# Half the tokens at a time from the first mixer to the choice of experts, and two token tiles' experts gathered

## The chip, the cores and the metric

The kernel runs on one core of one Trainium2 chip. The metric is device time in microseconds. A core has a matrix engine (TensorE, PE), a vector engine (VectorE, DVE), a scalar engine (ScalarE, ACT), a general engine (GpSimd, POOL), a queue engine (SyncE, SP) and 16 DMA engines. Every engine works through its own instructions in program order and waits for others by semaphores.

## The reference

Two transformer blocks over 512 tokens of width 1024, in fp32, cut to what matters here:

```python
# first block, modulated by mod = silu(c) @ w_mod + b_mod
h = rms_norm(x) * (1 + sc1) + sh1
x = x + 0.5 * gt1 * rms_norm(swiglu(h, w_gate1, w_up1, w_down1))      # 1024 -> 2816 -> 1024
u = rms_norm(x) * (1 + sc2) + sh2
x = x + gt2 * rms_norm(hybrid_mixer(u))        # attention on the top 128 keys of an indexer, dilated attention, gates
h = rms_norm(x) * (1 + sc3) + sh3
x = x + 0.5 * gt3 * rms_norm(swiglu(h, w_gate2, w_up2, w_down2))
# second block, modulated by silu(c_2) @ w_ada + b_ada
x = x + gt1 * (concat(mla(h), retention(h)) @ w_out)     # both causal: token t sees keys 0..t
h2 = rms_norm(x) * (1 + sc2) + sh2
# peer: 8 heads choose 16 of 16384 experts for every token
a = gelu(sum(expert_u[idx] * h2))              # 128 rows of 1024 a token
x = x + gt2 * sum((g * a) * expert_v[idx])
return rms_norm(x) * g_final
```

## The kernel before

**Tiles and products.** The 512 tokens are four tiles of 128 (t = 0 to 3). A product in fp32 is made of three matmuls in a reduced format (`mm3`, L124 to L128: high x high, high x low, low x high). Both operands are first cut into a high and a low part. For weights that is `split` (L116): a tile `raw` of 128 x 1024 comes by DMA, ACT copies it into `whi` (L120), DVE subtracts to get `wlo` (L121). Results that become operands go through `to_pair` (L130 to L132) in the same way.

**Stages.** `build` (L1585) runs, for all four tiles together: `begin` and the first `ffn` (L480; gate and up with 22 steps f, then down), `mixer1` (L652) and `combine1` (L965), `project` (L1015), the second `ffn`, `mixer2` (L1044), `project`, and then `peer` (L1403). Each weight is read and split once for the 512 tokens. At the end of a `project` or `ffn` stands a `boundary` (L435): join the sum to x, normalise each tile, transpose it.

**Modulation.** `mod_unit` (L256) multiplies a raw tile of 1 MB by the conditioning vector, in part on DVE (L283, L285, L297, tile `rows`) and in part on PE (L276). Such units are spread over the loops by `mods` (L305): 24 in the first ffn, 4 in `combine1`, 24 in the second ffn.

**Choice of experts.** `peer_queries`, `peer_level1` (L1253) and `peer_level2` (L1292) find 16 candidates of 128 keys in each half and then the best 16 pairs a head. For tile 0 the result is a list `ids` of 128 experts a token, fetched in 256 gathers: `gather` (L1452) issues an indirect DMA on POOL (L1458) that brings one row of 1024 for each of 128 tokens (512 KB) into `erow`. A gather from `expert_u` is followed by one DVE instruction (L1462) that multiplies by the token and sums; one from `expert_v` by a DVE instruction that adds it with its weight to `eacc` (L1470). Five buffers hold gathered rows.

**Dense experts.** For tiles 1 to 3 all 16384 experts are computed, in 128 chunks of 128. `emit_a` (L1430) multiplies a chunk of `expert_u` by the 384 tokens: 24 matmuls of 384 columns and a gelu. `peer_spread` (L1362) writes the chosen weights into a dense table `dg` in DRAM, 16 tokens a group, 24 groups, with compares on DVE (L1387 to L1390) and scatter matmuls (L1395). The dense loop (L1543) reads the table back (`gt`), multiplies, and adds the chunk of `expert_v` with 18 matmuls of 512 columns into `acc`. 78 chunks of `emit_a` run ahead, during the choice and the spread (`EARLY`); the results of 66 of them go out to DRAM (`da`) and come back. In the spread stage 0.7 gathers stand behind each chunk of `emit_a`, in the dense loop 0.85 to 2.6 behind each chunk (`R1` to `R4`). Where a gather stands is fixed by the program: `issue_after` puts it behind a named instruction.

## Time and profile before

| | |
|---|---|
| time, median of 3 runs (lowest to highest) | 2857.0 us (2856.21 to 2857.03) |
| the profiled execution, its own time | 2857.06 us |
| its span, first to last instruction | 2855.3 us |
| mean granted TensorE clock, share of 2.4 GHz | 0.987 |
| busy: PE, DVE, ACT, POOL | 2786.9, 2063.3, 1159.0, 368.6 us |
| DMA, mean over the span | 553.08 MB, 194 GB/s |

A busy engine is one with an instruction in it. Matmuls overlap in the array, so a busy PE is not PE at its peak; how close matmuls can follow one another is seen in their start times. The stages can be found in the timeline by the names of their tiles: start and first ffn to 402 us, first mixer and `combine1` to 921, projection and second ffn to 1302, second mixer and projection to 1598, queries and first choice to 1715, second choice, spread and the early chunks to 2095, dense loop to the end.

### The profile page before, as it was taken

Reading aid. Unit: us, or ns where it says so; the run is one execution under the profiler, and the core shown is the slowest. Engines: PE = TensorE matmul, PEld = TensorE weight load, DVE = VectorE, ACT = ScalarE, POOL = GpSimd, SP = SyncE. Lnnn points to the kernel's source line nnn. Section 1 sums busy time; section 2 is a strip of 40 time slices with the busy share of each in tenths; the row PEclk is TensorE's granted clock in tenths of the full one; section 3 lists DMA queues with packets and bytes.
Section 4 is the critical chain, followed back from the end, with each engine's and each line's share of the span. In section 5 each row is a group of like instructions: output and inputs, shape, how many; then the busy total and the mean of one; then the engine's idle time right before and its main releaser. Section 6 shows DMA issues by size and latency. Waiting matters only on the chain. (4 is left out here: it accounts for less than half of the span.)

```text
span 2855.3 us, 40921 instructions
## 1 busy us (share of the span) xinstructions
PE 2786.9 (98%) x15565; PEld 2394.8 (84%) x15565; DVE 2063.3 (72%) x4448; ACT 1159.0 (41%) x1930; POOL 368.6 (13%) x367
## 2 busy tenths in 40 slices
PE   8999999999999999999999999999999999999998
PEld 6877778869788877888898888999988888899996
DVE  6895257785656787226664789999967778887887
ACT  4343144333534444225522433655633333333333
POOL 0000000000000000001001002111121115443441
PEclk9999999999999999999997999999999999999999
DMA  6663221212033554321121226888899999888894
GB/s 274 224 232 140 94 84 60 93 60 89 16 139 139 188 225 178 110 103 42 67 79 47 103 90 216 310 281 309 322 333 338 327 313 362 314 311 319 295 334 189
DMA packets 152533, 553.08 MB, mean 194 GB/s; under 512 B 12368, under 2 KB 61840, under 8 KB 112400
## 3 DMA queue, kind: packets, MB, share of 16 engines
q1 hardware_dynamic: 111040, 404.25, 38.8%
q0 software_dynamic: 38848, 140.56, 13.8%
q10 hardware_dynamic: 2448, 5.65, 0.5%
q8 instruction: 122, 2.00, 0.3%
q14 instruction: 75, 0.61, 0.1%
HBM read 505.95 MB, written 44.47 MB: 193 GB/s over the span
## 5 line engine op out<-in xcount | busy, mean ns | idle before, releaser
L120 ACT ACTIVATE whi<-raw 128x1024 fp32r<-128x1024 f32 (+2 forms) x491 | 510.3, 1040 | 806.5 <-PE ps L127 377.3
L121 DVE TENSOR_TENSOR wlo<-raw,whi 128x1024 fp32r<-128x1024 f32 (+2 forms) x491 | 588.7, 1199 | 294.2 <-ACT whi L120 289.4
L126 PE MATMUL ps<-h_hi,whi 128*128 128x384 f32 (+2 forms) x1904 | 691.5, 364 | 4.6 <-ACT ga L1443 3.3
L127 PE MATMUL ps<-h_lo,whi 128*128 128x384 f32 (+2 forms) x1904 | 684.4, 360 | 0.9 <-DVE h_lo L132 0.9
L128 PE MATMUL ps<-h_hi,wlo 128*128 128x384 f32 (+2 forms) x1904 | 683.1, 359 | 1.6 <-DVE wlo L121 1.6
L126 PEld LDWEIGHTS ps<-h_hi,whi 128*128 128x128 f32 x1904 | 359.4, 189 | 37.7 <-ACT ga L1443 4.2
L128 PEld LDWEIGHTS ps<-h_hi,wlo 128*128 128x128 f32 x1904 | 359.1, 189 | 33.7 <-DVE wlo L121 2.4
L127 PEld LDWEIGHTS ps<-h_lo,whi 128*128 128x128 f32 x1904 | 359.7, 189 | 31.5 <-DVE h_lo L132 1.3
L126 PE MATMUL acc<-whi,wh 128*128 128x512 f32 x768 | 303.9, 396 | 1.6 <-ACT wh L131 1.6
L128 PE MATMUL acc<-whi,wl 128*128 128x512 f32 x768 | 303.9, 396 | 0.3 <-DVE wl L132 0.3
L127 PE MATMUL acc<-wlo,wh 128*128 128x512 f32 x768 | 303.7, 396 | 0.0
L1458 POOL DMA_INDIRECT erow<-in_eu,ids x128 | 142.8, 1116 | 649.3 <-DVE junk L1462 478.1
L131 ACT ACTIVATE wh<-wv 128x384 fp32r<-128x384 f32 x128 | 67.1, 524 | 339.4 <-issue 174.2
L1458 POOL DMA_INDIRECT erow<-in_ev,ids x128 | 166.7, 1302 | 222.7 <-DVE eacc L1470 197.0
L126 PE MATMUL ps<-whi,h_hi 128*128 128x256 f32 (+1 forms) x608 | 187.3, 309 | 0.0
L127 PE MATMUL ps<-wlo,h_hi 128*128 128x256 f32 (+1 forms) x608 | 185.3, 305 | 0.0
L128 PE MATMUL ps<-whi,h_lo 128*128 128x256 f32 (+1 forms) x608 | 185.2, 305 | 0.0
L128 PEld LDWEIGHTS acc<-whi,wl 128*128 128x128 f32 x768 | 144.5, 188 | 36.0 <-DVE wl L132 0.8
L126 PEld LDWEIGHTS acc<-whi,wh 128*128 128x128 f32 x768 | 144.3, 188 | 35.1 <-ACT wh L131 1.9
L127 PEld LDWEIGHTS acc<-wlo,wh 128*128 128x128 f32 x768 | 144.4, 188 | 32.9
L1470 DVE SCALAR_TENSOR_TENSOR eacc<-erow,wgt,eacc 128x1024 f32<-128x1024 f32 x127 | 162.7, 1281 | 4.0 <-DMA erow<-in_ev,ids 2.3
L285 DVE SCALAR_TENSOR_TENSOR rows<-mraw,sil,rows 128x256 f32<-128x256 f32 x336 | 160.3, 481 | 6.6
(457 smaller groups left out, 4602.9 us busy)
## 6 DMA issues: line engine op xcount, KB each, us to landing
raw<-in_euT SPq DMA_DIRECT2D x64, 1024.0 KB
raw<-in_evp SPq DMA_DIRECT2D x64, 1024.0 KB
raw<-in_gu SPq DMA_DIRECT2D x44, 1024.0 KB
mraw<-in_wmod SPq DMA_DIRECT2D x24, 1024.0 KB
mraw<-in_wada SPq DMA_DIRECT2D x24, 1024.0 KB
dg<-gb SPq DMA_DIRECT2D x24, 1024.0 KB
gt<-dg SPq DMA_DIRECT2D x16, 1536.0 KB
raw<-in_dn SPq DMA_DIRECT2D x22, 1024.0 KB
```

Source lines behind the costliest of these rows:

```text
L120: self.nc.scalar.activation(hi, r, AF.Copy)
L121: self.last_low = self.nc.vector.tensor_tensor(lo, r, hi.bitcast(F32), op=OP.subtract)
L126: mm(out, l[0], r[0], start=start, stop=False)
L127: mm(out, l[0], r[1], start=False, stop=False)
L128: self.last_mm = mm(out, l[1], r[0], start=False, stop=stop)
L131: self.nc.scalar.activation(hi, v, AF.Copy)
L285: nc.vector.scalar_tensor_tensor(rows, rv[:, k, :], c, rows, op0=OP.mult, op1=OP.add)
L1458: nc.gpsimd.indirect_dma_start(out=row, out_offset=None, in_=src, in_offset=bass.IndirectOffsetOnAxis(ap=ids[:, m:m + 1], axis=0))
L1470: nc.vector.scalar_tensor_tensor(eacc, row, wg[:, m:m + 1], eacc, op0=OP.mult, op1=OP.add)
```

## The change

From the first mixer on, tiles 0 and 1 go alone through `network(0)` (first mixer, `combine1`, `project_half`, `ffn_half`, second mixer, `project_half`) and `peer_level1`, 256 columns wide. Then tiles 2 and 3 go through `network(1)`. Each pass reads and splits all weights of these stages. Keys, values and the retention state of tiles 0 and 1 go to DRAM and come back for the second pass, since its tokens see them.

In the second pass a generator, `work_beside`, stands beside the network: first `peer_level2` of tiles 0 and 1, then 256 gathers from `expert_u`, each with its DVE product (L1563). `pull` takes its next piece behind every weight split (1.4 pieces in the mixers, 1.0 in the second ffn) and behind every step of the attention (0.8 or 0.5 of that). Four buffers (`slots`) hold these rows.

`peer` then treats tiles 2 and 3 as the dense ones: 24 matmuls of 256 columns and 12 of 512 a chunk, 16 groups. No gather of `expert_v` stands before the last loop: there `fetch` brings four gathers at a time, 0.7 fetches a chunk, into eight buffers, and `weigh` adds the rows with eight matmuls a fetch (L1711, weights of 32 columns) instead of DVE instructions.

The modulation units move: 34 in the first ffn, 4 in `combine1` and 14 in the second ffn, all in the pass of tiles 0 and 1.

```diff
+        self.pull(1.0, self.last_low)
         return hi, lo
+    def pull(self, n, after):
+        if self.beside is None:
+            return
+        self.owed += n * self.rate
+        with self.tc.issue_after(after.ins):
+            while self.owed >= 1:
+                self.owed -= 1
+                next(self.beside, None)
...
+    def ffn_half(self, b, gu, dn, h, late, between, join, scale, bias):
...
+                for t in range(0, 1 if f else 2):
+                    cut = slice(0, W) if f else slice(t * P, (t + 1) * P)
+                    late.pop(t, lambda: None)()
+                    for j in range(2):
+                        if len(ws) < 2:
+                            ws.append(self.split(r[:, j * 1024:(j + 1) * 1024]))
+                        w = ws[j]
+                        for k in range(KD):
+                            ks = slice(k * P, (k + 1) * P)
+                            self.mm3(p[:, j * W + cut.start:j * W + cut.stop], (w[0][:, ks], w[1][:, ks]),
+                                     (hi[:, k, cut], lo[:, k, cut]), k == 0, k == KD - 1)
...
+                    self.pull(0.8, self.last_neg)
...
+                if b:
+                    nc.scalar.dma_start(kT[:, :, :W], old["kT"])
+                    nc.scalar.dma_start(vv[:, :2], old["vv"])
+                    nc.scalar.dma_start(kix[:, :W], old["kix"])
...
+    def gather_u(self, n):
+        nc = self.nc
+        t, m = divmod(n, P)
+        row = self.slots[n % 4]
+        nc.gpsimd.indirect_dma_start(out=row, out_offset=None, in_=self.a["eu"],
+                                     in_offset=bass.IndirectOffsetOnAxis(ap=self.ids[t][:, m:m + 1], axis=0))
+        junk = self.misc.tile([P, D], BF, name="junk", tag="sg")
+        nc.vector.scalar_tensor_tensor(junk, row, 1.0, self.x(t), op0=OP.mult, op1=OP.mult,
+                                       accum_out=self.act[t][:, m:m + 1])
...
+            sel = yield from self.peer_level2(sp, v[t], ix[t])
+            nc.vector.scalar_tensor_tensor(self.idf32[t], sel[0], 128.0, sel[1], op0=OP.mult, op1=OP.add)
+            nc.vector.tensor_copy(self.ids[t], self.idf32[t])
+            nc.vector.tensor_copy(self.g0[t], sel[2])
+            yield
...
+        for n in range(2 * P):
+            self.gather_u(n)
+            self.got = n + 1
+            yield
...
-        NG = 24
+        NG = 16
         LEAD, EARLY = 12, 78
-        TAIL, FIN = 12, 4
-        R1, R2, R3, R4 = (0.7, 0.85, 2.6, 2.2)
+        FIN = 6
+        RU, RD, RW = 1.0, 2.0, 0.7
...
-                self.mm3(p[:, :384], (w[0][:, ks], w[1][:, ks]), (h[0][:, k, P:], h[1][:, k, P:]), k == 0, k == KD - 1)
+                self.mm3(p[:, :W], (w[0][:, ks], w[1][:, ks]), (h[0][:, k, :], h[1][:, k, :]), k == 0, k == KD - 1)
...
+        def fetch(k):
+            t, j = divmod(k, 32)
+            held[k] = [self.slots[(4 * k + g) % 8] for g in range(4)]
+            for g in range(4):
+                nc.gpsimd.indirect_dma_start(out=held[k][g], out_offset=None, in_=a["ev"],
+                                             in_offset=bass.IndirectOffsetOnAxis(ap=idt[t][:, 32 * g + j:32 * g + j + 1], axis=0))
...
+                for g in range(4):
+                    nc.tensor.matmul(y[t][hf][32 * g:32 * g + 32, :], z[:, j % 8, g, :], held[k][g][:, hf * 512:hf * 512 + 512],
+                                     start=j == 0, stop=j == 31)
...
+            owed += rate
+            while done < min(owed, 64):
+                with tc.issue_after(after.ins):
+                    fetch(done)
+                if done:
+                    with tc.issue_after(self.last_mm.ins):
+                        weigh(done - 1)
+                done += 1
...
-                for t in range(3):
+                for t in range(2):
...
-            gathers(R2 if c < EARLY - LEAD else R3 if c < P - LEAD else R4 if c < P - TAIL else 2 * P, pace)
...
+                values(RW if c < P - FIN - 2 else 99, pace)
...
+            self.mods(0 if not 1 <= f < 18 else 2)
...
+            if not self.tt[0]:
+                self.mods(0 if f < 1 else 1)
...
+                self.tt = (0, 1)
+                h, late = self.network(0, hs[0], late, old, rows, pn, between2)
...
+                    self.peer_level1(self.pool(s2, "sel1", reuse_waits="tile"), h, v, ix, late, lambda: None)
+                z = self.hbuf.tile([P, 4, D], F32, name="slots", tag="h_hi")
+                self.slots = [z[:, j] for j in range(4)]
+                self.put_away((0, 1))
...
+                self.beside = self.work_beside(sp, v, ix)
+                self.tt = (2, 3)
+                h, late = self.network(1, hs[1], [], old, rows, pn, between2, s1)
+            self.front.close()
+            self.peer(h, late, st)
```

Three places where the order changes. First, DVE in the gate and up loop of the second ffn; before, for all tiles (`rows` and `mc` are modulation, `av` the product of gate and up):

```order
L121 TENSOR_TENSOR wlo<-raw,whi 128x1024
L297 TENSOR_TENSOR rows<-rows,parts 128x256
L285 SCALAR_TENSOR_TENSOR rows<-mraw,sil,rows 128x256 x2
L283 TENSOR_SCALAR rows<-mraw,sil 128x256
L285 SCALAR_TENSOR_TENSOR rows<-mraw,sil,rows 128x256 x4
L517 TENSOR_TENSOR av<-ps,sg 128x512
L303 TENSOR_TENSOR mc<-mod,cols 128x2
L285 SCALAR_TENSOR_TENSOR rows<-mraw,sil,rows 128x256
L297 TENSOR_TENSOR rows<-rows,parts 128x256
L285 SCALAR_TENSOR_TENSOR rows<-mraw,sil,rows 128x256
L132 TENSOR_TENSOR alo<-av,ahi 128x512
```

After, in the pass of tiles 2 and 3:

```order
L122 TENSOR_TENSOR wlo<-raw,whi 128x1024 x2
L1563 SCALAR_TENSOR_TENSOR junk,act_3589<-slots,x_87 128x1024
L606 TENSOR_TENSOR av<-ps,sg 128x256
L1563 SCALAR_TENSOR_TENSOR junk,act_3589<-slots,x_87 128x1024
L144 TENSOR_TENSOR zlo<-av,zhi 128x256
L122 TENSOR_TENSOR wlo<-raw,whi 128x1024 x2
L1563 SCALAR_TENSOR_TENSOR junk,act_3589<-slots,x_87 128x1024
L606 TENSOR_TENSOR av<-ps,sg 128x256
L1563 SCALAR_TENSOR_TENSOR junk,act_3589<-slots,x_87 128x1024
```

The modulation is gone from this pass, the width is halved, the splits stay as they are, and a product with a gathered row (L1563) stands behind each split.

Second, POOL from the second norms to the last loop (`rstd` are small steps of norms). Before:

```order
L148 TENSOR_TENSOR rstd<-ssq,mhalf 128x1
L329 DMA grow<-drow 128x1024
L148 TENSOR_TENSOR rstd<-ssq,mhalf 128x1
L1489 IOTA iof 128x128
L1458 DMA erow<-in_eu,ids 128x1024 x128
L1458 DMA erow<-in_ev,ids 128x1024 x128
L1521 DMA fin<-dx 128x1024 x2
L329 DMA grow<-drow 128x1024 x2
```

After, first in the second pass:

```order
L1560 DMA slots<-in_eu,ids_3583 128x1024 x103
L160 TENSOR_TENSOR rstd<-ssum,mhalf 128x1
L160 TENSOR_TENSOR rstd<-ssq,mhalf 128x1
L160 TENSOR_TENSOR rstd<-ssum,mhalf 128x1
L344 DMA grow<-drow 128x1024
L160 TENSOR_TENSOR rstd<-ssq,mhalf 128x1
L1560 DMA slots<-in_eu,ids_3583 128x1024 x25
L1560 DMA slots<-in_eu,ids_3584 128x1024 x41
L160 TENSOR_TENSOR rstd<-ssum,mhalf 128x1
L160 TENSOR_TENSOR rstd<-ssq,mhalf 128x1
L160 TENSOR_TENSOR rstd<-ssum,mhalf 128x1
```

and later, at the way into the last loop:

```order
L1560 DMA slots<-in_eu,ids_3584 128x1024 x4
L1619 IOTA iof 128x128
L344 DMA grow<-drow 128x1024
L1560 DMA slots<-in_eu,ids_3584 128x1024 x17
L1643 IOTA eye 128x1024
L1661 DMA fin<-dx 128x1024 x2
L1691 DMA slots<-in_ev,idt_24376 128x1024 x4
L1691 DMA rows<-in_ev,idt_24376 128x1024 x4
```

Gathers now stand ahead of the norms of the pass in POOL's queue, and the gathers of `expert_v` behind everything else.

Third, PE in the dense loop; before, the products of values alone:

```order
L126 MATMUL acc<-whi,wh 128x512
L127 MATMUL acc<-wlo,wh 128x512
L128 MATMUL acc<-whi,wl 128x512
L126 MATMUL acc<-whi,wh 128x512
L127 MATMUL acc<-wlo,wh 128x512
L128 MATMUL acc<-whi,wl 128x512
```

After:

```order
L138 MATMUL acc<-whi,wh 128x512
L1711 MATMUL ga<-slots,zw 32x512 x8
L139 MATMUL acc<-wlo,wh 128x512
L140 MATMUL acc<-whi,wl 128x512
L138 MATMUL acc<-whi,wh 128x512
L139 MATMUL acc<-wlo,wh 128x512
L140 MATMUL acc<-whi,wl 128x512
L1711 MATMUL ga<-rows,zw 32x512 x4
```

The weighing of the gathered rows of tiles 0 and 1 stands among the dense products of tiles 2 and 3.

## Rows read from the trace of the kernel before

**Rows 1.** The page, part 2: traffic in GB/s in 40 equal slices
```profile
GB/s 274 224 232 140 94 84 60 93 60 89 16 139 139 188 225 178 110 103 42 67 79 47 103 90 216 310 281 309 322 333 338 327 313 362 314 311 319 295 334 189
```

**Rows 2.** Windows by stage: us, PE PEld DVE ACT POOL, PEclk, DMA, GB/s
```profile
402.00:921.00 519.00, 507.37 (x3048) 425.45 (x3047) 354.66 (x902) 226.40 (x491) 15.36 (x29) 0.99 0.23 79
921.00:1302.00 381.00, 376.50 (x1810) 305.33 (x1809) 231.99 (x425) 143.51 (x236) 5.54 (x10) 0.99 0.43 158
1302.00:1598.00 296.00, 281.78 (x2077) 260.69 (x2076) 181.04 (x500) 114.05 (x252) 23.52 (x43) 0.93 0.18 65
1598.00:1715.00 117.00, 113.61 (x620) 97.97 (x619) 98.99 (x499) 46.13 (x69) 2.86 (x5) 1.00 0.29 102
1715.00:2095.00 380.00, 370.08 (x2610) 357.11 (x2608) 349.35 (x901) 215.99 (x269) 62.75 (x54) 1.00 0.81 287
2095.00:2372.00 277.00, 276.12 (x1176) 222.11 (x1177) 219.81 (x324) 100.23 (x137) 61.52 (x61) 0.99 0.94 333
2372.00:2800.00 428.00, 428.00 (x2140) 384.61 (x2139) 350.56 (x370) 149.43 (x206) 186.84 (x144) 1.00 0.87 325
```

**Rows 3.** Timeline, PE, second ffn: start us, us, line, operation; 512 columns
```profile
1001.37 0.39 PE L126 MATMUL ps<-h_hi,whi 128*128 128x512 f32 x1
...
1003.41 0.39 PE L126 MATMUL ps<-h_hi,whi 128*128 128x512 f32 x1
```

**Rows 4.** Timeline, PE, first projection: first and last of 45 matmuls
```profile
878.81 0.28 PE L126 MATMUL ps<-whi,zh 128*128 128x256 f32 x1
...
883.99 0.28 PE L128 MATMUL ps<-whi,zl 128*128 128x256 f32 x1
```

**Rows 5.** Windows, tile wlo (splits), DVE busy, clock, DMA share, GB/s
```profile
402.00:1715.00 1313.00, 204.55 (x176) 0.98 0.28 101
1715.00:2095.00 380.00, 91.30 (x75) 1.00 0.81 287
```

**Rows 6.** Windows, tile rows (24 modulation units), DVE busy
```profile
921.00:1177.00 256.00, 104.91 (x240) 0.99 0.52 192
```

**Rows 7.** Waits of PE: us in total, times, longest us
```profile
PE ps L414 <- ACT xs L448: 15.3, 4, 4.9
```

**Rows 8.** Groups of DVE, products with gathered rows: busy, mean ns, idle before
```profile
L1462 DVE SCALAR_TENSOR_TENSOR junk<-erow,xr 128x1024 bf16<-128x1024 f32 x128 | 155.3, 1218 | 6.9 <-DMA erow<-in_eu,ids 6.9
```

**Rows 9.** Windows, tile erow, DVE, spread stage
```profile
1715.00:2095.00 380.00, 60.08 (x99) 1.00 0.81 287
```

**Rows 10.** Groups of DVE, spread stage: one of four alike
```profile
L1388 DVE TENSOR_TENSOR oj<-io,jt 128x1024 f16<-128x1024 f16 x48 | 32.8, 684 | 0.1
```

**Rows 11.** Short windows, columns as in rows 2
```profile
420.00:440.00 20.00, 14.94 (x109) 14.74 (x110) 11.81 (x27) 11.67 (x26) 4.08 (x9) 0.83 0.13 44
1617.50:1692.60 75.10, 75.10 (x373) 62.84 (x372) 68.70 (x395) 24.46 (x34) 0.00 (x0) 1.00 0.22 80
1797.00:1850.00 53.00, 53.00 (x447) 48.41 (x446) 52.56 (x80) 40.87 (x50) 6.21 (x6) 1.00 0.85 309
2120.00:2140.00 20.00, 20.00 (x87) 16.12 (x86) 16.36 (x24) 6.39 (x10) 3.90 (x5) 1.00 1.07 381
```

**Rows 12.** Tile erow on POOL: ns min/median/max, first and last start us
```profile
L1458 POOL DMA_INDIRECT erow<-in_eu,ids x128: 932/942/1976, 1752.6 to 2401.0; - x128
```

**Rows 13.** Groups of PE, spread stage: the scatter matmuls
```profile
L1395 PE MATMUL sc<-og,oi 128*128 128x128 f16 x768 | 53.8, 220 | 0.0
```

**Rows 14.** Timeline, PE, dense loop: first and last of 23 matmuls
```profile
2303.82 0.39 PE L127 MATMUL acc<-wlo,wh 128*128 128x512 f32 x1
...
2308.95 0.39 PE L128 MATMUL acc<-whi,wl 128*128 128x512 f32 x1
```

**Rows 15.** Timeline, PE: 32 modulation matmuls in groups of 32 columns
```profile
26.09 1.93 PE L276 MATMUL mod<-raw,cp 128*32 128x256 f32 x32
```

**Rows 16.** The page, part 3: hardware queue, packets, MB, share of 16 engines
```profile
q1 hardware_dynamic: 111040, 404.25, 38.8%
```

**Rows 17.** Timeline, PE: the last matmul of the span
```profile
2844.35 0.40 PE L128 MATMUL acc<-whi,wl 128*128 128x512 f32 x1
```

More of the change, by code (lines that the diff above doesn't have):

```diff
@@ L22 @@
 S = 512
+W = 256
 NT = 4
@@ L556, in nform @@
         kh = 1024 // width
-        out = [self.ps() for _ in range(NT)]
+        nt = len(self.tt)
+        late = dict(late or ())
+        wait = bool(late)
+        out = [self.ps() for _ in range(nt)]
         ws = []
@@ L571, in nform @@
             ws = []
-        for t in range(NT):
+        for t in range(nt):
             then(t, out[t][:, :width])
@@ L595, in attend @@
         l, r, masks, vals = seg
-        w = r.shape[-1]
+        w = sum(z.shape[-1] for z in r)
         got = {}
@@ L600, in first @@
             p = self.ps("ps")
-            nc.tensor.matmul(p[:, :w], l, r, start=True, stop=not masks)
+            c = 0
+            for i, z in enumerate(r):
+                nc.tensor.matmul(p[:, c:c + z.shape[-1]], l, z, start=True, stop=i < len(r) - 1)
+                c += z.shape[-1]
             for m, (c0, mk) in enumerate(masks):
@@ L725, in dsa_prep @@
         pki = self.ps("po")
-        for t in range(NT):
+        for t in range(2):
             c = pa[:, t, 256:640]
@@ L753, in indexer @@
         nc = self.nc
-        for i in range(1, NT):
+        for l, i in enumerate(self.tt):
+            if not i:
+                continue
             w = (i + 1) * P
@@ L1472, in peer @@
-        self.owed = 0.0
-        self.got = 0
-        def gathers(n, after):
-            self.owed += n
-            with tc.issue_after(after.ins):
-                while self.got < 2 * P and self.got < self.owed:
-                    gather(self.got)
-                    self.got += 1
         nxt = 0
@@ L1628, in residual, with run @@
+    def run(self, steps):
+        while True:
+            try:
+                next(steps)
+            except StopIteration as e:
+                return e.value
     def residual(self, t, y, grow):
```

742 lines of the change are left out of this document (434 added, 308 removed).

## The prediction

> **What bounds the kernel now.** I read four views. First the traffic over the span [rows 1]: after the first quarter it falls to 16 to 200 GB/s for a third of the time and then stands above 280 to the end. So the stretch from the first mixer to the choice of experts has DMA to spare, and the dense stretch has not.
>
> Then the windows, one for each stage [rows 2]: first mixer and its combination 519 us, second ffn with its projection 381, second mixer 296, queries and first choice 117, spread 380, dense loop 277 + 428 and its end. In each TensorE is busy 95 to 100% of the time. From the pitch of its matmuls (starts of 10 in a row, 2.04 us: 0.227 us for 512 columns [rows 3]; starts of 45 in a row, 5.18 us: 0.118 for 256 [rows 4]; 22 steps in 5.13 us: 0.233 in the dense loop [rows 14]) its work can be added up. DVE is busy 61 to 92% in the same windows: it is not the bound, but not idle either.
>
> So before, TensorE bounds nearly everything. The question is what bounds each stage when half of the tokens pass at a time and the gathers stand elsewhere.
>
> **Start and first ffn (to 402 us).** The work is the same for four tiles; modulation units move forward into it, ten more than before. TensorE pays for each 32 matmuls in four column groups, 1.93 us [rows 15], of which part lies beside other work: +3 us, 405 us (0 to +20).
>
> **First pass, tiles 0 and 1.** The stages from 402 to 1715 took 519 + 381 + 296 + 117 = 1313 us [rows 2]. What streams tokens halves: 656 us. Additions:
> - Where weights are stationary and 512 tokens stream, two matmuls of 256 take 2 x 0.118 = 0.236 us for 0.227 [rows 3, 4]. About 2,000 such matmuls (1,056 in the gate and up products, 384 each for gates and queries, 144 and some): 18 us in two passes, 9 in this one.
> - 14 modulation units stand in this pass's second ffn, one for each step of its gate and up loop. A unit is 4.37 us of DVE (104.91 us for 24 [rows 6]), a split 1.16 to 1.22 us (204.55 us for 176 [rows 5]; 91.30 for 75 there). With two splits a step is 2.4 + 4.4 = 6.8 us of DVE against 48 x 0.118 = 5.65 of TensorE: 14 x 1.15 = 16 us, where DVE was covered before by twice the matmuls.
> - At a boundary TensorE waits for the normalised tile, 15.3 us in four waits [rows 7]. With two tiles there is less of the next tile's product to cover it: three boundaries of 3.8 us, 11 us.
> Sum 692 us. Ends: 655 (all additions covered) and 740 (each stage as badly filled as the worst of rows 2, 95%, and boundaries doubled).
>
> **Second pass, tiles 2 and 3, with the gathers.** TensorE needs the same 656 + 9. But DVE has more. In the four windows it was busy 354.66 + 231.99 + 181.04 + 98.99 = 867 us [rows 2]. Of that 204.6 are splits of weights [rows 5], which don't halve since each pass reads and splits the weights again; 28 x 4.37 = 122 are modulation [rows 6], gone from this pass; half of the remaining 540 is 270. So 475 us without anything beside it. (In the first pass it is 475 + 18 x 4.37 = 554, under TensorE's.) The change adds
> - 251 of the 256 products of a gathered row of expert_u with the token, as the order shows, at 1.218 us [rows 8]: 306 us;
> - the second choice for tiles 0 and 1. In the spread stage DVE was busy 349.35 us [rows 2], of which 91.3 splits [rows 5], 60.1 products with gathered rows [rows 9] and 4 x 32.8 = 131.2 of spreading ([rows 10], one of four equal lines): 67 us left for four tiles, 17 each, 34 us.
> 475 + 306 + 34 = **815 us of DVE** against 665 of TensorE. DVE becomes the bound of this pass. How full can it get? Where it had the most work it was busy 68.70 of 75.1 us and 52.56 of 53.0 [rows 11], 91% and 99%. At 94% the pass takes 867 us; at 99%, 823. The upper end is another wait: on POOL about 20 small steps of the norms stand in the same queue as the gathers (a gather is 0.94 us of POOL [rows 12]), and a gather waits for the product four earlier, so a norm can stand behind a gather that waits for DVE. 20 norms at up to 3 us are 60: 930 us. I take 867, since both of the fullest windows are short. DMA has room: 251 x 0.524 MB on top of the pass's own, about 104 MB (133 MB of 101 GB/s over 1313 us [rows 5], less 29 MB of modulation), is 236 MB in 867 us, 272 GB/s.
>
> **Spread stage.** It was 380 us for 76 chunks at 24 matmuls of 384 columns. Now it is 76 x 24 x 0.118 = 215 us, and two thirds of the 53.8 us of scatter matmuls [rows 13], 36: with some others 258 us. DVE has, by the same rows, 91 + 2 x (17 + 44) + 10 = 223 us. TensorE is the bound and two choices stand at its head: 270 us (258 to 290). That is a gain of 110 us.
>
> **Dense loop.** Before it is 760 us (2095 to 2855.3), bound by TensorE: 18 matmuls of 0.233 a chunk, and 24 more in the chunks that still have keys to multiply. Now a chunk has 12, 2.80 us, and the keys' part is 24 x 0.118 = 2.82. But all 256 gathers of expert_v stand in this loop, 0.7 x 4 a chunk up to chunk 91, where the loop before held the 128 gathers of v and part of u. Bytes: a gather is 128 x 1024 x 4 = 0.524 MB, a chunk of dense values 0.524, the weights 0.131, the kept products 0.131. Chunks 0 to 65: 0.524 + 0.131 + 0.131 + 2.8 x 0.524 = 2.254 MB. The hardware queue moved 404.25 MB in 38.8% of 2855.3 us, 365 GB/s when all engines move [rows 16]; the window from 2095 had 333 at a share of 0.94 [rows 2], 354. I take 360: 6.26 us a chunk. TensorE needs 2.80 + 0.7 x 0.96 = 3.5 there (a fetch is weighed by 8 matmuls of 512 columns in groups of 32, 0.12 each after rows 15), so **DMA is the bound**: 66 x 6.26 = 413 us. Chunks 66 to 91 read keys too (0.524) but no kept products: 2.647 MB, 7.35 us, x 25.4 = 187 us. Chunks 92 to 115 have TensorE as bound, 24.6 x 5.62 = 138; the last 12, 34; start 3 and end 11 (the last matmul started at 2844.35 [rows 17]). Sum 786 us. The best stretch of the trace, 381 GB/s [rows 11], gives 754; 333 gives 836.
>
> **Sum.** 405 + 692 + 867 + 270 + 786 = 3020, and the 1.8 us that the profiled execution (2857.06) had around its span (2855.3): **3022 us**. That execution is the median of the runs (2857.0), so nothing is to be shifted. Against before: two passes with re-read weights and gathers +246, spread -110, loop +26, start +3.
>
> **Rivals.**
> 1. *The dense loop isn't bound by DMA (faster than before).* If all transfers stay hidden, the loop is TensorE's: 66 x 3.5 + 25.4 x 6.3 + 186 = 577 us, the total 2813. For it: before, the loop kept TensorE at 100% while DMA stood at 0.87 to 0.94 [rows 2], so queues share well. Against: chunks 0 to 91 hold 216 MB; 577 us asks 555 GB/s of them. With the other stages as forecast the change pays from 500 GB/s; with all at their lower ends (655, 823, 258) from 400. The best window is 381 at a share of 1.07 [rows 11], so no row shows it. The Trainium skill, DMA: Bandwidth & Descriptors, section Measured, gives 425 GB/s for large transfers on one core with its neighbour idle, as here. By that the loop is an estimated 696 us and the total 2932; no window here reaches it, and the trace decides.
> 2. *The clock falls where TensorE now waits (slower still).* From 420 to 440 us it was busy 14.94 of 20 us, waiting in pieces, and its granted clock was 0.83, between the 1.2 and 2.4 GHz levels; in the second mixer 0.93 [rows 2, 11]. In the second pass and in chunks 0 to 65 it would be busy 77% and 56% of the time. If half of the pass runs at the lower level, it has 656 x 1.5 = 984 us at worst and some 947 with overlap, +80; in the loop 2 x 3.5 = 7.0 instead of 6.26, +49: 3150 us. The Trainium skill, TensorE: Matmul & The Clock Gate, section HAM oscillation, describes the same for bursts of matmuls between waits for DMA; rows 11 show one such stretch, none a long one.
> 3. *The gathers don't run beside the second pass as written.* If a gather's wait and POOL's single queue let each norm stall until the gathers ahead have landed, the products bunch, DVE idles and then blocks: the pass is near the plain sum, 665 + 306 = 971, total 3126.
>
> **How the numbers follow.** Forecast 0.62 (2900 to 3110 by its ends), rival 2 0.19, rival 1 0.10, rival 3 0.06; 0.03 for a sum of low ends that ends level. Each low end taken together gives 405 + 655 + 823 + 258 + 754 = 2895 us, still slower than before. Leaving out rival 1 and the upper part of rival 2, the range is 2910 to 3170. A measurement of this kernel tells 0.2% (6 us) from no change: faster 0.10, same 0.03, slower 0.87.
>
> **What would show it.** In the profile after: first pass 655 to 740 us with TensorE over 90% busy; second pass with DVE at 90% or more and TensorE near 77%, its waits ending on weight splits; spread near 270 with TensorE bound; chunks 0 to 91 with a DMA share near 1, TensorE waiting for the value rows or gathers, 6 to 7 us a chunk. Wrong would be: DVE under 85% in the second pass (then POOL or the clock is the reason), or chunks of 4 us at over 450 GB/s.

## The result and the profile after

The changed kernel takes 3380.6 us, median of 4 runs (3368.4 to 3398.6), against 2857.0 us before: a ratio of 1.184, 95% interval 1.178 to 1.189. It is slower, as forecast, but by 524 us and not by 165, and it lies above the range, which ended at 3170. The profiled execution took 3368.4 us, its span 3366.6; it is the fastest of the four, and all that is read from a trace below is compared with it.

First the page, part 2, in 40 slices of 84 us (busy tenths, granted clock, DMA share, GB/s); the line that answers it is [rows 1]:

```profile
PE   8999989879978888786799778789999999999998
DVE  6994377559566698987688787789743333323456
PEclk9999999879989797897799888799999999999999
DMA  7674234447533332678699676657989988888863
GB/s 279 242 250 142 88 118 151 156 151 275 196 132 96 130 126 96 227 253 280 227 322 335 234 261 214 224 185 261 315 287 325 319 310 295 322 282 292 324 216 138
```

The clock is no longer flat: from slice 8 to slice 26 it is often at seven or eight tenths. DVE stands at nine in two slices alone of the second pass (slices 15 to 26). And in the dense loop, from slice 30, DMA stands at eight to nine tenths while DVE falls to three.

The windows by stage, columns as in [rows 2]: first pass, second pass, spread, dense loop.

```profile
402.00:1204.00 802.00, 712.86 (x4820) 657.80 (x4819) 548.60 (x1371) 372.85 (x714) 34.68 (x57) 0.90 0.44 153
1204.00:2225.00 1021.00, 820.60 (x4955) 722.97 (x4955) 821.81 (x1954) 347.98 (x612) 335.51 (x295) 0.84 0.67 232
2225.00:2489.00 264.00, 254.83 (x2309) 246.97 (x2309) 214.47 (x462) 168.66 (x228) 2.22 (x3) 0.99 0.76 264
2489.00:3366.00 877.00, 861.15 (x3771) 487.58 (x3769) 346.41 (x463) 246.04 (x370) 262.58 (x262) 0.99 0.81 285
```

| stage | before, halved where two passes share it | forecast | measured |
|---|---|---|---|
| start and first ffn | 402 | 405 | 402 |
| first pass, tiles 0 and 1 | 656 | 692 | 802 |
| second pass, tiles 2 and 3 | 656 | 867 | 1021 |
| spread | 380 | 270 | 264 |
| dense loop to the end | 760 | 786 | 877 |

Three terms carry the miss: +110, +154 and +91. The other two hold within 6 us. In the first pass TensorE is busy 713 of 802 us at a mean clock of 0.90, in a pass that has no gathers. In the second, DVE is busy 822 us, as summed (815), but that is 80% of the pass and not 94%. In the loop TensorE is busy 861 of 877 us: that points to it as the bound, where DMA was forecast; e3 to e5 below test it.

The work of TensorE at full pitch can be summed from the trace (for each form of matmul the lower quartile of the time from its start to the next start, times its count): an estimate of 644 us in the first pass and 681 in the second; in the four stages before 1204, half of which is 602. What is over splits by whether the next matmul started without a gap (slow clock and switches) or after one:

| | work | without a gap | at gaps |
|---|---|---|---|
| half of the stages before | 602 | 36 | 19 |
| first pass | 644 | 58 | 100 |
| second pass | 681 | 116 | 224 |

So it is above all waiting that came on top, in both passes, then a slower clock, and then some 40 us of work.

What TensorE waited for in the first pass (us in total, times, longest us):

```profile
PE ps L138 <- ACT half L143: 23.0, 6, 5.6
PE ps L315 <- ACT parts L310: 13.1, 3, 5.0
PE ps L437 <- ACT xs L473: 13.1, 4, 4.9
```

The pairs `half` and the tiles `xs` are the boundaries; `parts` are the casts of the modulation in the first combination. Its timeline, rows with a wait alone:

```profile
638.42 0.18 PE L315 MATMUL ps<-oneb,parts 128*128 128x1 bf16 x1 [3.44 <-ACT parts L310]
645.61 0.58 PE L138 MATMUL ps<-half,whi 128*128 128x256 f32 x1 [2.37 <-ACT whi L121]
661.57 0.18 PE L315 MATMUL ps<-oneb,parts 128*128 128x1 bf16 x1 [4.69 <-ACT parts L310]
```

The combination (617 to 727 us) is made of short products between steps of the other engines; the three rows show waits of 2 to 5 us between them. In the second pass the waits are for weights:

```profile
PE ps L139 <- DVE wlo L122: 44.5, 27, 7.5
PE ps L138 <- ACT whi L121: 29.3, 11, 7.9
PE ps L140 <- DVE wlo L122: 25.6, 24, 6.4
```

and those of ScalarE, which makes their high parts, for the tiles that DMA brings:

```profile
ACT whi L121 <- DMA raw<-in_gu: 65.7, 19, 6.5
ACT whi L121 <- DMA raw<-in_wg: 40.3, 9, 10.2
ACT whi L121 <- DMA raw<-in_dn: 35.1, 10, 5.4
```

DVE, which was to be the bound of this pass, waited in turn for ScalarE and for gathered rows:

```profile
DVE wlo L122 <- ACT whi L121: 58.1, 21, 7.6
DVE av L606 <- ACT sg L604: 24.9, 20, 2.7
DVE junk L1563 <- DMA slots<-in_eu,ids: 24.7, 21, 3.2
```

In the dense loop the timeline of TensorE shows the weighing of gathered rows (`ga`):

```profile
2599.92 1.90 PE L1711 MATMUL ga<-rows,zw 128*32 128x512 f32 x4
2601.76 0.50 PE L138 MATMUL acc<-whi,wh 128*128 128x512 f32 x1
...
2603.59 1.90 PE L1711 MATMUL ga<-rows,zw 128*32 128x512 f32 x4
2605.43 0.50 PE L139 MATMUL acc<-wlo,wh 128*128 128x512 f32 x1
...
2607.26 1.92 PE L1711 MATMUL ga<-slots,zw 128*32 128x512 f32 x8
2609.11 0.50 PE L140 MATMUL acc<-whi,wl 128*128 128x512 f32 x1
```

A weighing matmul leaves two records: the program has 512 of them and the trace 1,024, while a dense product leaves one. The eight records in 1.85 us are four matmuls, and the four records in 1.84 us two. The modulation's 32 records [rows 15] are, by the program, 16 matmuls of 256 columns, so one of 512 columns in a group of 32 has 0.24 us there and not 0.12; and here a fetch of eight takes 1.85 + 1.84 + 1.84 us and not 0.96.

### The profile page after: what moved, and what is told of

The parts are those of the page before. It is cut to its first block, busy times and chain, and to the rows that moved or that the text cites. A ratio compares the mean times of both kernels' runs of the same rounds, so it can differ in the third digit from the quotient of the medians.

```text
span 3366.6 us, 46843 instructions
## 1 busy us (share of the span) xinstructions
PE 3034.7 (90%) x17758; PEld 2407.1 (72%) x17758; DVE 2200.3 (65%) x4822; ACT 1288.7 (38%) x2188; POOL 639.2 (19%) x628
## 4 chain that ended last, share of the span: by engine, by line
PE 61%; DVE 16%; DMA 10%; issue 7%; ACT 4%; POOL 2%; ACTq 0%; POOLq 0%; DVEq 0%; SPq 0%
PE ps L138 11%; PE ps L140 11%; PE ps L139 11%; PE ga L1711 9%; PE acc L138 4%; PE acc L140 4%; PE acc L139 4%; DVE wlo L122 4%; DMA slots<-in_eu,ids 2%; DMA raw<-in_gu 2%; DVE junk L1563 2%; ACT whi L121 2%; DMA raw<-in_dn 1%; PE ps L686 1%; POOL slots L1560 1%
## 5 line engine op out<-in xcount | busy, mean ns | idle before, releaser
L122 DVE TENSOR_TENSOR wlo<-raw,whi 128x1024 fp32r<-128x1024 f32 (+2 forms) x681 | 808.7, 1193 | 439.0 <-ACT whi L121 425.8
L121 ACT ACTIVATE whi<-raw 128x1024 fp32r<-128x1024 f32 (+2 forms) x681 | 699.9, 1031 | 908.9 <-PE ps L139 379.9
L138 PE MATMUL ps<-half,whi 128*128 128x256 f32 (+1 forms) x2304 | 696.9, 303 | 51.6 <-ACT half L143 25.7
L140 PE MATMUL ps<-half,wlo 128*128 128x256 f32 (+1 forms) x2304 | 689.1, 300 | 30.1 <-DVE wlo L122 30.1
L139 PE MATMUL ps<-half,whi 128*128 128x256 f32 (+1 forms) x2304 | 687.9, 299 | 1.0 <-DVE half L144 1.0
L138 PEld LDWEIGHTS ps<-half,whi 128*128 128x128 f32 x2304 | 474.8, 206 | 74.1 <-ACT whi L121 29.6
L140 PEld LDWEIGHTS ps<-half,wlo 128*128 128x128 f32 x2304 | 473.6, 206 | 48.1 <-DVE wlo L122 36.5
L139 PEld LDWEIGHTS ps<-half,whi 128*128 128x128 f32 x2304 | 474.8, 206 | 12.4 <-issue 8.4
L1560 POOL DMA_INDIRECT slots<-in_eu,ids x256 | 305.6, 1194 | 599.7 <-DVE junk L1563 426.7
L1563 DVE SCALAR_TENSOR_TENSOR junk<-slots,x 128x1024 bf16<-128x1024 f32 x256 | 310.4, 1218 | 37.7 <-DMA slots<-in_eu,ids 24.7
L139 PE MATMUL ps<-wlo,half 128*128 128x256 f32 (+1 forms) x608 | 203.0, 335 | 38.0 <-DVE wlo L122 37.9
L138 PE MATMUL ps<-whi,half 128*128 128x256 f32 (+1 forms) x608 | 196.1, 333 | 32.2 <-ACT half L143 17.2
L140 PE MATMUL ps<-whi,half 128*128 128x256 f32 (+1 forms) x608 | 199.4, 329 | 0.0
L1711 PE MATMUL ga<-slots,zw 128*32 128x512 f32 x512 | 168.1, 599 | 2.6 <-DMA slots<-in_ev,idt 2.6
L1711 PE MATMUL ga<-rows,zw 128*32 128x512 f32 x512 | 168.0, 598 | 0.2 <-DMA rows<-in_ev,idt 0.2
```

The source lines that it names most:

```text
L121: self.nc.scalar.activation(hi, r, AF.Copy)
L122: self.last_low = self.nc.vector.tensor_tensor(lo, r, hi.bitcast(F32), op=OP.subtract)
L138: mm(out, l[0], r[0], start=start, stop=False)
L139: mm(out, l[0], r[1], start=False, stop=False)
L140: self.last_mm = mm(out, l[1], r[0], start=False, stop=stop)
L1560: nc.gpsimd.indirect_dma_start(out=row, out_offset=None, in_=self.a["eu"], in_offset=bass.IndirectOffsetOnAxis(ap=self.ids[t][:, m:m + 1], ...
```

## Experiments

All stages below are read from three marks that each trace has: the first and the last key product of the choice of experts (tile `pq`, the first in tiles 0 and 1's, the last in tiles 2 and 3's) and the first dense product (tile `acc`). For the changed kernel, with first and last start at the end of the row's numbers:

```profile
L1417 PE MATMUL sc<-sk,pq x128: 275/275/582, 1144.4 to 2216.3; 128*128 128x128 f32 x128
```

| run | time, us | first pass (from 402) | second pass | spread | loop |
|---|---|---|---|---|---|
| the changed kernel, profiled | 3368.4 | 742 | 1072 | 273 | 877 |
| e1, no gathers of u | 3171.8 | 740 | 887 | 268 | 873 |
| e2, gathers of u without products | 3248.1 | 744 | 957 | 267 | 877 |
| e10, half products | 3319.1 | 744 | 1024 | 270 | 878 |
| e11, plain loads, no products | 3245.9 | 754 | 944 | 267 | 878 |
| e9, gathers of u at half pace | 3429.0 | 748 | 932 | 468 | 877 |
| e3, no weighing | 3223.4 | 743 | 1062 | 275 | 741 |
| e4, no gathers of v | 3138.1 | 742 | 1074 | 274 | 644 |
| e5, weighing in one block | 3266.0 | 743 | 1073 | 275 | 771 |
| e6, third weight buffer | 3355.1 | 724 | 1073 | 278 | 876 |
| e7, no modulation in the combination | 3352.7 | 725 | 1072 | 275 | 877 |
| e8, added matmuls | 3392.8 | 767 | 1069 | 276 | 878 |
| e12, e5 + e6 + e7 | 3219.6 | 712 | 1061 | 273 | 770 |
| e13, no norms at boundaries | 3324.6 | 723 | 1047 | 275 | 876 |

(The marks put the first choice of tiles 0 and 1, some 60 us, into the second pass, in all rows alike. The experiments are one run each, beside 2855.4 to 2861.4 us of the kernel before; stages that an edit doesn't touch repeat within 12 us of the first row, so a difference of that size in a stage says nothing.)

**Theories.** The prediction's: the second pass is bound by DVE's work, the passes are else halves, the loop is bound by DMA. The rival that the profile suggests: half-width stages leave TensorE waiting whatever stands beside them, and the loop is bound by TensorE through the weighing.

### e1: the second pass without gathers

```diff
-        for n in range(2 * P):
-            self.gather_u(n)
-            self.got = n + 1
-            yield
+        for t in range(2):
+            nc.vector.memset(self.act[t], 0.5)
+        self.got = 2 * P
```

> Leaves out the 256 gathers of expert_u and their products (the activations are a constant); the second choice of experts stays beside the second pass. The changed kernel took 802 us in the first pass, 1021 us in the second (1204 to 2225). If the half-width passes themselves leave TensorE waiting (theory 1), the second pass comes down to about the first one's level: 802 less some 20 for the modulation that only the first one has, plus 17 to 34 for the second choice on DVE: 790 to 830 us, total about 3160. If DVE work is the bound of the second pass and the pass is else half of the whole-width stages (the prediction's theory), it comes to 665 to 700 us, total about 3040.

Window of its second pass:

```profile
1204.00:2037.00 833.00, 749.53 (x4973) 675.29 (x4976) 544.43 (x1437) 350.12 (x611) 25.14 (x37) 0.91 0.37 124
```

833 us, near the first pass's level and far from 665 to 700. With 544 us of DVE in it, DVE is no bound there. The half-width pass alone, with the second choice of tiles 0 and 1 beside it, costs 177 us more than half of the stages before; the gathers and their products 188. Split as above it has 678 us of work, 60 without a gap and 95 at gaps, which is the first pass over again.

### e2, e10, e11: what of a gather costs

```diff
-        nc.vector.scalar_tensor_tensor(junk, row, 1.0, self.x(t), ...)          # e2, e11: left out
+        nc.vector.scalar_tensor_tensor(junk[:, :512], row[:, :512], 1.0, ...)   # e10
-        nc.gpsimd.indirect_dma_start(out=row, ..., in_=self.a["eu"], ...)
+        nc.gpsimd.dma_start(row, self.a["eu"][(n % P) * P:(n % P + 1) * P, :])  # e11
```

> Leaves out the products of the gathered rows of expert_u on DVE; the 256 gathers stay where they are (the activations are a constant). If it is DVE's 310 us of products that lengthen the second pass, it takes what it takes without gathers, within 20 us. If it is the transfers (134 MB beside the weights) or the place of the gathers in POOL's queue, it stays within 60 us of 1021.

> Leaves out half of each product of a gathered row of expert_u (512 of 1024 columns), some 0.55 us of DVE each, 140 us in all. Leaving out the whole product gave 114 us (1021 to 907). If DVE's time is what counts, the second pass gets 50 to 80 us shorter. If it is the place in DVE's queue, a product that waits for a landing row and holds the splits behind it, it gets less than 25 us shorter.

> As the run without products, but with 128 rows in a row loaded by plain DMAs in place of the gathers: the same bytes from the same engine without the 0.94 us of POOL for each. With gathers and without products the second pass took 907 us, without gathers 833. If these 74 us are the transfers beside the weights (waits of ScalarE for weight tiles grew most), it stays at 890 to 910. If POOL's queue is the reason, it falls to 833 to 850.

Neither expectation for e2 came true: the pass fell to 907 us, between them. Its window, and ScalarE's wait for the second ffn's weights:

```profile
1204.00:2111.00 907.00, 788.58 (x4989) 699.45 (x4991) 548.26 (x1460) 350.70 (x616) 302.02 (x295) 0.87 0.72 263
```

```profile
ACT whi L121 <- DMA raw<-in_gu: 48.3, 18, 4.5
```

So the gathers alone cost 70 us (957 against 887) and the products 115. Half the product takes 0.68 us instead of 1.22 and gives back 48 of these 115 (e10): what counts is DVE's time, about in proportion, although DVE is not full: 251 products of 1.22 us are 306 us, of which a third and more comes through. Plain loads of the same bytes cost 57 us of the 70 (e11): most of it is the transfers beside the weight tiles, and not the time of a gather on POOL. Nor did norms stand long behind gathers in POOL's queue: in the second pass of the changed kernel all waits of other engines for POOL's `rstd` make 13.1 us, none over 1.4, and without gathers (e1) 13.2. The longest of these sums:

```profile
DVE pn L504 <- POOL rstd L160: 3.1, 4, 1.4
```

Without gathers the longest sum of waits of ScalarE for a weight tile was 17.5 us:

```profile
ACT whi L121 <- DMA raw<-in_wd: 17.5, 7, 6.2
```

and none for the second ffn's was above 5; with them it waited 48 us for these alone.

### e9: half the pace

```diff
-        self.rate = 1.4        # mixers; 1.0 in the second ffn
+        self.rate = 0.7        # 0.5
```

> The pace of the gathers of expert_u beside the second pass is halved (0.7, 0.5 and 0.7 pieces a split instead of 1.4, 1.0 and 1.4): some 105 stand in the pass, 96 in the spread stage, 55 at the start of the dense loop. Without any the pass took 833 us, with 251 of them 1021. If what they cost there is in proportion to their number, the pass takes 905 to 920 us; the spread stage gets 96 x 1.22 = 117 us of DVE on top of 226 in 264 us and becomes 340; the loop, in which the gathers of expert_v start 28 chunks later, stays within 30 us of 877: total 3330 to 3370. If the cost in the pass is one of a few bad waits, it falls by less than 40.

By the starts of the products in the trace, 110 of the 256 stood in the pass, 146 in the spread stage and none in the loop; the expectation had 105, 96 and 55. The pass fell by 140 us, more than in proportion (107), but the spread stage grew by 195 where 76 were expected, and the total by 60. Its window, from the last key product to the first dense product:

```profile
2081.00:2550.00 469.00, 327.48 (x2365) 305.95 (x2366) 385.43 (x779) 174.29 (x235) 198.93 (x147) 0.84 0.85 309
```

DVE at 82%, DMA at 0.85, TensorE at 70% and a clock of 0.84: with 146 products there, the spread stage has the second pass's state. A gather of u with its product cost 0.75 us in the pass (188 us for 251) and 1.35 us in the spread stage (195 for the 144 that came on top).

### e3, e4: the loop without weighing, and without gathers

```diff
-            for hf in range(2):
+            for hf in range(2) if j in (0, 31) else ():     # e3: of the weighing, the first and last fetch of a tile
-            for g in range(4):
-                nc.gpsimd.indirect_dma_start(out=held[k][g], ..., in_=a["ev"], ...)   # e4
```

> Leaves out the weighing matmuls of 60 of the 64 fetches of expert_v; all 256 gathers stay. The dense loop took 877 us (2489.6 to the end) with TensorE busy all the time and a DMA share of 0.9. If TensorE is its bound through the weighing (8 records in 1.85 us for half a fetch, 3.7 us a fetch, against 0.96 in the prediction), the loop falls to the DMA bound of the prediction, 770 to 800 us, with a DMA share near 1. If the transfers are the bound already, it stays at 865 to 880.

> Leaves out the 256 gathers of expert_v in the dense loop; the weighing stays, on rows that are there already. If TensorE is the bound of the loop, it stays within 20 us of 877. If the transfers are, it falls to what TensorE needs by the prediction, 575 to 620 us. If both are needed (weighing waits for rows that come late), it falls in between, with TensorE still at over 95%.

Two windows of e3's loop, then one of e4's:

```profile
2600.00:2700.00 100.00, 51.21 (x192) 39.73 (x192) 31.86 (x48) 22.57 (x32) 52.73 (x52) 0.74 1.03 400
2900.00:3000.00 100.00, 80.21 (x483) 71.80 (x484) 44.88 (x56) 36.54 (x56) 56.38 (x49) 0.88 1.03 409
```

```profile
2600.00:2700.00 100.00, 99.42 (x552) 58.42 (x551) 55.08 (x81) 34.33 (x53) 0.72 (x2) 1.00 0.59 191
```

Without weighing the loop takes 741 us, 30 less than the lower end expected, and in these windows DMA is the bound (share 1.03, 400 and 409 GB/s), with TensorE waiting at a clock of 0.74 to 0.88. Over the 610 us in which e3 gathers, the mean is 374:

```profile
2490.00:3100.00 610.00, 434.70 (x2143) 351.41 (x2142) 258.55 (x355) 187.88 (x280) 272.16 (x253) 0.85 0.97 374
```

Without gathers the loop takes 644 us, and TensorE is full. So in the changed kernel TensorE was the bound through the weighing; there it waited next to nothing for gathered rows:

```profile
PE ga L1711 <- DMA slots<-in_ev,idt: 2.6, 3, 1.8
```

But 644 lies far below 877 although all weighing is in it: left alone, the weighing is cheap. The timeline of e4 shows why:

```profile
2540.50 1.92 PE L1709 MATMUL ga<-rows,zw 128*32 128x512 f32 x16
2542.35 0.50 PE L138 MATMUL acc<-whi,wh 128*128 128x512 f32 x1
```

Sixteen records, a whole fetch, in 1.85 us: the four column groups work at once, and the row after it starts 1.85 us later. In the changed kernel it took three times as long. The order of its instructions has the answer, the same in 54 of the 64 fetches (9 stand whole, one in other pieces); TensorE, dense loop, the second fetch:

```
L1711 MATMUL ga<-rows,zw 32x512 x4
...
L1711 MATMUL ga<-rows,zw 32x512 x2
...
L1711 MATMUL ga<-rows,zw 32x512 x2
```

The eight matmuls of a fetch stand as 4, 2 and 2 among the dense ones, each piece behind the gathered rows that it needs. A gathered row has two matmuls, one for each half of it, and both use the same 32 columns. In the changed kernel one alone took 0.97 us from its start to the next:

```profile
2844.00 1.04 PE L1711 MATMUL ga<-slots,zw 128*32 128x512 f32 x2
2844.97 0.50 PE L140 MATMUL acc<-whi,wl 128*128 128x512 f32 x1
```

Two with the same columns took 1.84 us, as long as all eight: the four groups run side by side, the two matmuls of a group one after the other.

### e5: the same eight in one block

```diff
+            rr = (self.z4, self.rows4)[k % 2]
+            zk = gp.tile([P, 4, 32], F32, name="zk", tag="zk", bufs=2)
+            nc.vector.scalar_tensor_tensor(zk, rr[:, :, 0:32], 0.0, y["w"][:, j % 8], op0=OP.mult, op1=OP.add)
-                    nc.tensor.matmul(y[t][hf][...], z[:, j % 8, g, :], held[k][g][...])
+                    nc.tensor.matmul(y[t][hf][...], zk[:, g, :], held[k][g][...])
```

> One thing changes in the changed kernel: the eight weighing matmuls of a fetch take their weights from a small DVE copy that reads a piece of all four gathered rows, so that all eight stand together on TensorE, behind the last of the four gathers. In the changed kernel's order they stand as 4, 2 and 2, each piece behind its own gather, and the same 32 columns twice in a row. Without gathers the weighing ran in groups of four, 1.85 us a fetch. If the order breaks the overlap of the four column groups, the loop is no longer bound by TensorE (2.80 + 0.7 x 2.05 = 4.2 us a chunk) and falls from 877 us to what the transfers need, 730 to 745 (730 without weighing), total 3215 to 3240. If the landing rows themselves slow the weighing, it stays at 850 or more.

The loop falls to 771 us and the kernel to 3266.0; its 64 fetches stand whole and take 1.85 us at the median, with the rows landing as before. A block, a window, and TensorE's wait:

```profile
2607.19 1.92 PE L1714 MATMUL ga<-rows,zk 128*32 128x512 f32 x16
2609.05 0.50 PE L140 MATMUL acc<-whi,wl 128*128 128x512 f32 x1
```

```profile
2600.00:2700.00 100.00, 81.05 (x410) 46.67 (x402) 42.29 (x69) 26.08 (x38) 44.03 (x44) 0.91 1.02 390
```

```profile
PE ga L1714 <- DVE zk L1711: 92.5, 33, 7.8
```

Now DMA is the bound: a share of 1.02, 390 GB/s, and TensorE waits 92.5 us for the copy `zk`, which comes behind the last row of a fetch. The expected 730 to 745 was some 30 us too low: transfers ran at 390 GB/s here and at 400 in the same window of e3. The rival (landing rows slow the weighing) is out.

### e6, e7: buffers and modulation in the first pass

```diff
+            self.third, self.n_raw = self.pool(st, "wraw3a"), 0      # e6, around combine1 and around mixer2
-            self.mods(1 if n >= NG1 else 0, tag="ps")                # e7
```

> A third buffer for weight tiles in both passes, from the first combination to its projection and in the second mixer and its projection (the first mixer has no room for it). In the first pass these stretches (617 to 752 and 927 to 1137 us) took 345 us for some 216 of TensorE at its full pitch. If TensorE waits there for weights that are loaded too late, two buffers being too few for half the work per weight, both passes get 40 us shorter or more, total 3290 or less. If the waits are round trips between engines (TensorE, ScalarE, DVE and back), they get less than 15 us shorter each.

> The four modulation units of the first combination move into the second ffn (18 there instead of 14). In the first pass the combination took 110 us (617 to 727) for 63 of TensorE, and TensorE waited for the modulation's parts three times, 13.1 us, behind a chain of nine DVE steps, three casts and six small matmuls. If that chain is what makes the combination long, it falls to 80 to 90 us and the second ffn grows by 5: total 20 us less. If it is the other chains of half-width stages, it falls by less than 10.

The marks of e6 and of e7:

```profile
L1417 PE MATMUL sc<-sk,pq x128: 275/275/582, 1126.0 to 2199.2; 128*128 128x128 f32 x128
```

```profile
L1416 PE MATMUL sc<-sk,pq x128: 275/275/582, 1126.9 to 2198.8; 128*128 128x128 f32 x128
```

e6 gave 18 us in the first pass and nothing in the second, short of its 40: in the stages that got the third buffer late loads are a small part. The ffns and the first mixer were not tried. e7 gave 17 us, near the 20 expected.

### e8: added work against the clock

```diff
+        for _ in range(self.warm):        # 4 behind each split in mixers, combination and projections
+            self.nc.tensor.matmul(d, self.idb, self.masks[:, 0:4, :]...)
```

> Adds work: four matmuls of 512 columns of constants (about 0.21 us each) behind each weight split in both mixers, combinations and projections, 760 in all or 162 us of TensorE in both passes, and one bank less for the rest. In the first pass the granted clock was 0.89 to 0.91, in the second 0.80 to 0.88. If the half clock after short waits is a large part of the loss (up to 80 us of the first pass's 156 over its full-pitch work), the clock comes up to 0.95 or more and the passes stay at 802 and 1021 within 20 us or get shorter, in spite of the added work. If it is the waits themselves, the added work makes each pass 50 to 80 us longer.

Its two passes:

```profile
402.00:1228.00 826.00, 772.39 (x5199) 674.12 (x5198) 553.85 (x1371) 375.86 (x714) 34.33 (x57) 0.94 0.43 148
1228.00:2245.00 1017.00, 857.44 (x5333) 719.86 (x5331) 820.80 (x1953) 349.08 (x612) 331.34 (x295) 0.90 0.68 233
```

The clock rose from 0.90 to 0.94 and from 0.84 to 0.90. The first pass got 25 us longer and the second 3 us shorter, with about 80 us of work added to each. So the answer lies between. Split as above, the first pass has 78 us more work, 42 less at gaps and 12 less without a gap; the second 81 more, 50 less and 34 less. Much of the added work went into gaps, and of the slow clock's time the runs gave back 12 and 34 us; no pass was shorter by more than 3 us. The clock has a part in the loss, in the first pass a small one. That it only follows the waits is argued, not shown: e8 fills gaps and raises the clock at once.

### e12: three edits together

> Three changes together: the weighing of a fetch as one block, the third weight buffer, no modulation in the first combination. Alone they gave 106 us in the loop, 18 and 17 in the first pass. If they are independent, the total is 3376 - 141 = 3235 us, within 20, still far above the kernel before; if the buffer and the modulation save the same wait, 3250.

```profile
L1416 PE MATMUL sc<-sk,pq x128: 275/275/582, 1113.7 to 2174.5; 128*128 128x128 f32 x128
```

3219.6 us, as expected within 16: within the noise the three add up, and together they are 149 of the 511 us between the two profiled executions. It doesn't come near the kernel before.

### e13, e14: the same chain at half and at whole width

```diff
-            r = self.xrstd(t)
+            r = self.ones[:, 0:1]          # and the same in postnorm; e13 after, e14 before
```

> Leaves out, in both half-width passes, the sums of squares and roots of the norms at the three boundaries (behind the first combination's projection, the second ffn and the second mixer's projection): the tiles are scaled by one instead. In the first pass TensorE waited 13.1 us for normalised tiles and 23.0 us for the pairs that follow them. If chains of small steps that half the tiles no longer cover are what the passes wait for, each pass gets 15 to 25 us shorter. If the waits have other reasons, less than 8 each.

> The same left out of the kernel before, at its three whole-width boundaries. If four tiles cover each other's norm steps there, it gets less than 10 us faster in all (2857 to 2847 or more). If it gets 20 us faster or more, the norms cost the same at either width, and half width doesn't expose them.

The marks of e13 and of e14 (before had its first and last key product at 1615.7 and 1715.6 us):

```profile
L1420 PE MATMUL sc<-sk,pq x128: 275/275/582, 1125.3 to 2171.9; 128*128 128x128 f32 x128
```

```profile
L1285 PE MATMUL sc<-sk,pq x128: 270/275/377, 1609.3 to 1709.2; 128*128 128x128 f32 x128
```

At half width the norms of three boundaries cost 19 us in the first pass and 25 in the second. At whole width all three together cost 7 (2851.2 us against 2858.1 beside it). The same steps for the same four tiles cost some six times as much in two passes: four tiles cover them, two don't. (The 25 are the less certain, since the second pass repeats within 12.)

## Why the prediction was wrong

- **Direction and structure held.** Slower was forecast at 0.87. Start (402 for 405) and spread (264 for 270, with TensorE busy 97%) came out. The start's +3 us had no ground: its rows 15 are of matmuls that only the first eight modulation units have, not the ten that moved, and the term measured nothing. DVE's sums were right: 549 us in the first pass for 554, 822 in the second for 815.
- **The first pass: "What streams tokens halves: 656 us".** This step failed, and e1 shows the same excess in the second pass (833 us without gathers). What halves is the streaming; the round trips between engines don't: norm, cast, transpose, pair, split. The additions of 36 us priced single places, and 146 were measured: by the split above 42 us of work (9 forecast), 81 of gaps and 22 of slower clock and switches. The runs show 18 of them for buffers (e6), 17 for the modulation's chain (e7) and some 15 for norms (19 in e13, less half of the 7 in e14; the forecast had 11 for the waits at boundaries, read from the normalised tiles alone). The rest, some 95, was not taken apart; that its gaps are of the same kind is argued from the waits, not shown.
- **The second pass: "DVE becomes the bound of this pass", "At 94% the pass takes 867 us".** The sum of DVE's work was right, the filling was not: 80%. The two windows taken for it [rows 11] lie in the choice and the spread stage, where DVE stood idle for 6.4 and 0.4 us. Here its work comes in turns with ScalarE, DMA and TensorE, and it waited 58 us for high parts of weights alone. Without any gather the pass is 833 us with DVE at 65% (e1), so DVE is not what bounds it; gathers add 70 us and products 115 (e2). For DVE under 85% the prediction named POOL or the clock as the reason. POOL it wasn't (13.1 us of waits); the clock was a part (e8).
- **The transfers: "DMA has room", 272 GB/s.** Over the mean, yes; but the gathers alone cost 70 us (e2), 57 of them as plain loads too (e11), and ScalarE's waits put them on weight tiles that came late. A mean share of 0.67 did not make a transfer free.
- **The loop: "0.7 x 0.96 = 3.5" and "DMA is the bound".** The price of a fetch was wrong twice. 32 records of modulation were taken for 32 matmuls; they are 16, which gives 1.85 us a fetch (e4). And the eight were taken to stand together, though the order ahead of the prediction shows pieces of four behind the first fetch: 5.5 us. With 5.53 the prediction's own sum has TensorE as the bound, 6.7 us a chunk up to chunk 65 and 9.5 up to 91, and gives 867 us for the 877 measured. With the order mended (e5) the loop is bound by DMA and takes 771 us, for a forecast of 786. That this is so near is in part luck: by the starts of `acc` chunks 0 to 65 took 353 us for 413 forecast, and chunks 66 to 91 took 232 for 187.
- **Rivals.** The first (loop not bound by DMA, so faster) had it half right: it wasn't DMA, but TensorE was slower, not faster. Three windows of 100 us or more in e3 moved 400 to 409 GB/s, above the 381 that the trace of before had shown; the mean over e3's gathers was 374, near the forecast's 360. The Trainium skill, DMA: Bandwidth & Descriptors, section Measured, has 425 GB/s; no window here reached it, and the mean of this mix of gathers and loads stayed well below. The second (clock) happened in the passes, at 0.90 and 0.84, beside waits that cost more (e8), and in the loop only where DMA was the bound (e3, e5). The Trainium skill, TensorE: Matmul & The Clock Gate, section HAM oscillation, describes such bursts between waits; the runs agree in kind, at 0.84 and 0.90 on the mean of a pass. The third (bunched products, 971 us for the pass) was closest to the second pass's number, but not by its reason: the waits for POOL's norm steps made 13.1 us.
- **The range** missed since three terms lay above their own upper ends (802 for 740, 1021 for 930, 877 for 836). Each end was a guess of how one resource fills, and none allowed that TensorE and DVE could both stand at 80% in one pass.

## What to carry to other kernels

Halving the tokens that pass at a time halves the streaming, but not the chains of small steps around it: look up what stands between the streams (norms, splits, evictions, modulation), and price it as exposed unless a second tile's work is shown to cover it. "Add up each engine's work and take the largest" is a lower bound; in a stage where the engines take turns, two of them can stand at 80%, and work put beside it on an engine that isn't full then costs a good part of its own time (here 115 of 306 us). Matmuls in column groups ran side by side here only when they stood together; when a wait for data splits a group, look at the order, and give the group one common wait. And before a price is read from a trace, count its records against the matmuls of the program.

## What the runs showed of the hardware

- Eight fp32 matmuls of 512 columns in four groups of 32 columns, two to a group, took 1.85 us in one block (e4, e5); four in two groups took 1.85, two with the same columns 1.84, and one 0.97 us (the changed kernel).
- Each of these matmuls left two records, a dense product one.
- A core moved 400 and 409 GB/s over 100 us each, at a DMA share of 1.03, with gathers and loads mixed, and 374 on the mean of 610 us (e3).
- The granted clock was 0.74 on the mean of 100 us in a loop that waited for DMA in pieces (e3).
